# Tying two modulation units behind the last activation of each feed-forward part

## The chip, the cores and the metric

The kernel runs on one core of one Trainium2 chip. TensorE (PE) multiplies matrices, VectorE (DVE) and ScalarE (ACT) work element by element, GpSimd (POOL) does little here, and SyncE (SP) issues the transfers (DMA) that bring weights from the chip's main memory into the core's own. Each engine works through its own list of instructions in order; semaphores tie the lists together. The metric is the time of one execution on the device in microseconds (us). The kernel before takes 2133.24 us, the median of three runs (2132.33 to 2133.75).

## What is computed

The reference is an encoder trunk of two layers on 512 tokens of width 1024. Each layer is a feed-forward half-step, a token mixer and another feed-forward half-step; the mixer is a state-space scan in the first layer and differential attention in the second. Cut to what matters here:

```python
cond = silu(c)
for i in range(DEPTH):
    mods = (cond @ ada_w[i] + ada_b[i]).reshape(b, N_SUB, 3, D_MODEL)
    gate = lambda s: (1 + mods[:, s, 2])[:, None, :]
    y = swiglu(modulate(x, mods[:, 0]), ffn_w_gate[i, 0], ffn_w_up[i, 0], ffn_w_down[i, 0])
    x = layer_norm(ALPHA * x + 0.5 * gate(0) * y, ln_g[i, 0], ln_b[i, 0])
    ...
    y = swiglu(modulate(x, mods[:, 2]), ffn_w_gate[i, 1], ffn_w_up[i, 1], ffn_w_down[i, 1])
    x = layer_norm(ALPHA * x + 0.5 * gate(2) * y, ln_g[i, 2], ln_b[i, 2])
```

with `swiglu(u) = (silu(u @ w_gate) * (u @ w_up)) @ w_down`, D_FF = 2816.

## The kernel before

**Arithmetic.** Everything is float32, but TensorE is fed a rounded format (F32R). Each operand x is therefore split into a high part (ScalarE copies x into the rounded format) and a low part (VectorE subtracts the high part from x), and each product is three matmuls: high by high, high by low, low by high (`mm3`, L182). So every weight and every activation costs ScalarE one instruction and VectorE one: L123 and L126 for weights, L155 and L156 for activations (`split_act`, which calls `split_into`).

**The feed-forward layers** (`ffn`, called with n = 0, 2, 3 and 5; here the first to the fourth feed-forward layer). The 2816 hidden columns are 22 blocks of 128, in three parts of 8, 7 and 7 blocks. In a part, the kernel first makes the activations of its blocks one after another and appends their split forms to the list `hs`; then come eight down units (`down_units`), one for each 128 output columns. A down unit loads its weight, splits it, multiplies it with all activations of the part (7 or 8 blocks by three matmuls, the last activation last in program order), and adds the result to the residual (L415). The first ten blocks of the first layer and the first four of the others are done by plain projections; the remaining ones by `seven`, a scheme with seven half-size products in place of eight. Its weights are added and split on VectorE and ScalarE (`weight_forms`, L543, L544 and L553), and its activation comes out of a short chain: L590 on VectorE, a SiLU on ScalarE (L591), a product on VectorE (L592), and the split. The inputs of `seven` need split sums of the layer's input as well (`input_forms`); these are made beside the last four plain blocks, and they too go through `split_act`.

**The modulation units** (`ada_unit`, L207). The vector `mods` is computed on VectorE, off the matmul path: one unit loads 128 rows of 1024 weights (512 KB), multiplies them with the conditioning vector and sums along the row, one instruction and a short one that reads the sum. There are 72 units for each of the trunk's two layers. A generator issues them a few at a time: in the first feed-forward layer two after each down unit of the first two parts and one after each of the third; in the second and the third layer two after each down unit of the first two parts; some others beside the activations. The fourth has none.

**Buffers and loads** (`load`, L99). All weights, those of the modulation units too, go through one kind of buffer. Four belong to one pool; inside the feed-forward layers every fifth load uses a buffer of its own. SyncE issues the loads. A buffer is free again once the last instruction that reads it has run: the split of a weight, or the modulation unit itself.

**What sets the order.** The order of each engine's list is not that of the program text. A planner at compile time goes through the instructions by their place in the program, with costs for each, and gives an engine the next instruction that is ready in its own simulated time. So a modulation unit whose weights have come early, while VectorE has nothing else ready, is put ahead of work that stands before it in the program. An order can be forced with `add_manual_dep(a, b, NOSYNC)`: a is not put ahead of b. Between two instructions of one engine that needs no semaphore.

Of the kernel before, what the change touches and what calls it, by code (L numbers as in the profile page):

```python
# [43 lines left out]
NOSYNC = mybir.DependencyInfo(mybir.DependencyClass.NoSync, mybir.DependencyReason.DATA)  # L44


def hybrid_trunk(tc, xT, cb, par, cst, adaw, wgu, wdn0, wdn1, wdn2, wdt, win, wso, wqk, wv, wao, dist_in, dtp, lam_in, out):
    nc = tc.nc
# [13 lines left out]
    def big(dt=F32, name="big"):  # L62
        return ap.tile([P, T], dt, tag="a", name=name)

    def tmp(name="tmp"):
        return tp.tile([P, T], F32, tag="t", name=name)

    def acc(tag="acc"):
        return ps.tile([P, T], F32, tag=tag, name=tag, bufs=BANKS[tag])
# [19 lines left out]


    fifth, at, last_load, hold_split = [None], [0], [None], [None]

    def load(src, n=1024):
        at[0] = (at[0] + 1) % 5
        if fifth[0] is not None and at[0] == 0:
            raw = fifth[0].tile([P, 1024], F32, tag="raw5", name="raw", bufs=1)
        else:
            raw = wp.tile([P, 1024], F32, tag="raw", name="raw", bufs=4)
        last_load[0] = nc.sync.dma_start(raw[:, :n], src)  # L99
        return raw[:, :n]  # L100
# [46 lines left out]

    def split_act(src, scale=None):
        hi, lo = big(F32R, "hi"), big(F32R, "lo")
        split_into(hi, lo, src, scale)  # L150
        return hi, lo

    def split_into(hi, lo, src, scale=None):
        if scale is None:
            x = nc.scalar.activation(hi, src, AF.Copy)  # L155
            y = nc.vector.tensor_tensor(out=lo, in0=src, in1=hi.bitcast(F32), op=ALU.subtract)  # L156
            return x, y
        else:
            nc.scalar.activation(hi, src, AF.Copy, scale=scale)
            nc.vector.scalar_tensor_tensor(  # L160
                out=lo, in0=src, scalar=scale, in1=hi.bitcast(F32), op0=ALU.mult, op1=ALU.subtract
            )
# [30 lines left out]
    def proj(o, w, u, m=P, cols=FULL, prev=None, lows_last=False):  # L193
        for a, b in cols:
            prev = mm3(
                o[:m, a:b], [(w[k][0], w[k][1], u[k][0][:, a:b], u[k][1][:, a:b]) for k in range(len(u))], prev,
                lows_last=lows_last,
            )
        last_mm[0] = prev
        return prev  # L200
# [3 lines left out]

    def ada_unit(l, j):
        raw = load(adaw[l, j])
        nc.vector.scalar_tensor_tensor(  # L207
            out=raw, in0=raw, scalar=1.0, in1=cond, op0=ALU.mult, op1=ALU.mult,
            accum_out=mods[l][:, j : j + 1],
        )  # L210

    onep, shift, gvec, lnG, lnB, lnag, lnab = {}, {}, {}, {}, {}, {}, {}

# [34 lines left out]
    def ada_stream(l, js):  # L248
        for j in js:
            ada_unit(l, j)  # L250
            if (j + 1) % 8 == 0:
                s, ty = divmod(j // 8, 3)
                n = l * 3 + s
                if ty == 1 and n > 0:
                    make_shift_scale(n)
                elif ty == 2:
                    make_gate(n)
            yield

    def advance(g, n):  # L260
        for _ in range(n):
            if g is None or next(g, "end") == "end":
                return
# [145 lines left out]
    def scale_residual(k=KT):  # L409
        for f in later[:k]:  # L410
            f()
        del later[:k]

    def add_res(d, pd, n, a, b):
        nc.vector.scalar_tensor_tensor(  # L415
            out=res[d][:, a:b], in0=pd[:, a:b], scalar=gvec[n][:, d : d + 1], in1=res[d][:, a:b],
            op0=ALU.mult, op1=ALU.add,
        )
# [3 lines left out]
    def first_units(n):  # L422

        if n == 1:
            src = [win[e] for e in range(2)]
        elif n == 4:
            src = [wqk[0, e] for e in range(2)]
        else:
            src = [wgu[{2: 1, 3: 2, 5: 3}[n], j // 2, j % 2] for j in range(3)]
        return [split(load(x), "a") for x in src]  # L430

    def down_units(n, u, units, ln=None, KEEP=4):

        last = ln is not None
        keep = []
        for ld in units:
            for d, w in ld():
                if last and d >= KT - KEEP:
                    keep.append((d, w))
                    continue  # L440
                pd = acc()
                proj(pd, w, u)
                add_res(d, pd, n, 0, T)
                if last:
                    ln.feed(d, 0, T)
            yield
        if last:
            finish(n, ln, [(d, w, u) for d, w in keep])

    def finish(n, ln, keep, begun={}):  # L450

        norm = None
        for a, b in HALVES:
            for d, w, u in keep:
                if a == 0 and d in begun:
                    pd, k0 = begun[d]
                    last_mm[0] = mm3(pd[:, a:b], [(*w[k], *(x[:, a:b] for x in u[k])) for k in range(k0, len(u))], start=False)
                else:
                    pd = acc()
                    proj(pd, w, u, cols=((a, b),))  # L460
                add_res(d, pd, n, a, b)
                ln.feed(d, a, b)
                advance(norm, 2)
            advance(norm, KT)
            norm = ln.normalize(a, b, ln.stats(a, b))
        advance(norm, KT)
        next_u[0] = ln.u
        ln.residual()
# [127 lines left out]
    def ffn(n, stream=None, per=(0, 0, 0), pre=None, first7=FT):  # L596


        forms, making = [], None
        ln, shifting = LN(n), None  # L600
        sc = ExitStack()
        extra[0] = fifth[0] = sc.enter_context(tc.tile_pool(name=f"wx{n}", bufs=3))
        idx = {0: 0, 2: 1, 3: 2, 5: 3}[n]
        u = next_u[0]
        f = 0
        pre = pre or first_units(n)
        for pi, nf in enumerate(FPARTS):
            hs = []
            open7 = None
            for _ in range(nf):  # L610
                if f >= first7:
                    g = seven(load(wgu[idx, f, 0]), load(wgu[idx, f, 1]), forms, hs)
                    next(g)
                    advance(shifting, 1)
                    if open7 is not None:
                        next(open7, None)
                    next(g)
                    open7 = g
                    f += 1
                    continue  # L620
                wg, wu = (pre.pop(0) if pre else split(load(wgu[idx, f, e])) for e in range(2))
                cols = HALVES if f < 2 and n > 0 else FULL
                tag = "mid" if f == 2 else "ln" if f == 3 and n == 0 else "acc"
                pg = acc(tag)
                proj(pg, wg, u, cols=cols, lows_last=f < 1 and n > 0)
                pu = acc(tag)
                proj(pu, wu, u, cols=cols, lows_last=f < 1 and n > 0)
                sg = tmp("sg")
                nc.scalar.activation(sg, pg, AF.Silu)
                h = tmp("h")  # L630
                nc.vector.tensor_tensor(out=h, in0=sg, in1=pu, op=ALU.mult)
                hs.append(split_act(h))
                if first7 - 4 <= f < first7:
                    making = making or input_forms(u)
                    forms.append(next(making))
                f += 1
                scale_residual(2 if f < 5 else KT)
                if f > 3 or n > 0:
                    advance(stream, per[0])

            if open7 is not None:
                next(open7, None)

            def mk(d):
                return lambda: [(d, split(load(wdn[pi][idx, d], nf * P)))]

            for _ in down_units(n, hs, [mk(d) for d in range(KT)], ln if pi == len(FPARTS) - 1 else None):
                advance(stream, per[1 if pi < 2 else 2])
            if pi == len(FPARTS) - 2:
                shifting = ln.shift()  # L650
        extra[0] = fifth[0] = None
        sc.close()
# [612 lines left out]
    for d in range(KT):  # L1265
# [9 lines left out]
        for o in (hl[0], uf):  # L1275
            x = nc.scalar.activation(o, res[d], AF.Identity, bias=shift[0][:, d : d + 1], scale=onep[0][:, d : d + 1])
# [8 lines left out]
    next_u[0] = up  # L1285
    st0 = ada_stream(0, range(16, 72))
    ffn(0, st0, (2, 2, 1), [[k[j] for k in ks] for j in range(8)], first7=10)
    advance(st0, 100)
    ssm(1)
# [108 lines left out]
```

## Time and profile before

| | |
|---|---|
| median of three runs | 2133.24 us |
| the profiled execution | 2134.65 us |
| its span, first to last instruction | 2132.8 us |
| TensorE busy in the span | 2099.9 us |
| VectorE busy | 1770.3 us |
| ScalarE busy | 1093.8 us |
| modulation units on VectorE, 144 of them | 173.7 us |

All are of one execution except the median. "Busy" of TensorE counts a matmul from its start to a modelled end, and matmuls overlap. The granted clock of TensorE was 0.997 of full speed in this execution. In the views below, a row of a timeline reads: start in us from the span's start, length in us, engine, line, operation, output and inputs by the program's names, shapes, count, and in brackets the engine's idle time before it with what ended it. A row of the chain of waits reads: start, length, what the end of the program was waiting for at that time. A row of a list of waits reads: who waited for whom, us in total, how often, the longest. The row of a group reads: line, engine, operation, names, shapes, count, then busy time in us, mean length in ns, and the engine's idle time before it. Of a transfer it gives KB each and the median time from issue to landing in us.

### The profile page before, as it was taken

How to read it: one execution, taken by the hardware profiler on the slowest of the kernel's cores; microseconds unless marked ns; L12 is line 12 of the kernel's file. 1: busy time of each engine (PE TensorE's matmuls, PEld its weight loads, DVE VectorE, ACT ScalarE, POOL GpSimd, SP SyncE). 2: the span in 40 equal slices, each digit the busy share in tenths (PEclk: the TensorE clock that was granted, in tenths of full speed). 3: DMA queues.
4: the chain of work that ended last, by engine and by line, in shares of the span. 5: the costliest groups of instructions: out<-in, count | busy, mean ns of one | idle time of the engine just before them, and what ended most of it. 6: DMA issues, size and time to landing. Idle time of an engine off the chain costs nothing.

```text
span 2132.8 us, 34111 instructions
## 1 busy us (share of the span) xinstructions
PE 2099.9 (98%) x13234; PEld 1854.1 (87%) x13234; DVE 1770.3 (83%) x2932; ACT 1093.8 (51%) x1833; POOL 180.6 (8%) x258
## 2 busy tenths in 40 slices
PE   7999999999999999999999999999999999999998
PEld 6889899976777699899999989899988888989897
DVE  6979998677667898989988989997788889858796
ACT  5424354777656646343456434353866647424343
POOL 0000000056333400000000000000011100000000
PEclk9999999999999999999999999999999999999999
DMA  8863735375554352727343373723322322323231
GB/s 321 306 227 99 247 97 195 93 214 170 151 152 135 92 159 72 271 91 238 123 144 104 106 240 103 253 96 113 92 69 80 90 81 78 124 75 119 71 118 40
DMA packets 90274, 301.19 MB, mean 141 GB/s; under 512 B 10240, under 2 KB 13696, under 8 KB 90112
## 3 DMA queue, kind: packets, MB, share of 16 engines
q1 hardware_dynamic: 88576, 294.81, 42.6%
q0 software_dynamic: 1536, 4.20, 0.9%
q8 instruction: 104, 1.70, 0.3%
q14 instruction: 58, 0.48, 0.1%
HBM read 289.53 MB, written 5.24 MB: 138 GB/s over the span
## 4 chain that ended last, share of the span: by engine, by line
PE 85%; DVE 7%; DMA 2%; issue 2%; ACT 2%; POOL 1%; SPq 0%; POOLq 0%; ACTq 0%; DVEq 0%
PE acc L182 68%; PE mid L182 9%; PE mid L909 2%; PE mid L1142 1%; DVE raw L207 1%; PE ln L182 1%; DMA raw<-in_adaw 1%; DVE raw L553 1%; DVE wl L544 1%; DMA raw<-in_wdn 1%; PE ln L1164 1%; PE ln L847 0%; POOL E L899 0%; DVE wl L126 0%; PE ln L339 0%
## 5 line engine op out<-in xcount | busy, mean ns | idle before, releaser
L182 PE MATMUL acc<-hi,wh 128*128 128x256 f32 (+1 forms) x1568 | 522.0, 334 | 1.8 <-ACT hi L155 1.8
L182 PE MATMUL acc<-lo,wh 128*128 128x256 f32 (+1 forms) x1568 | 521.8, 333 | 0.6 <-DVE lo L156 0.6
L182 PE MATMUL acc<-hi,wl 128*128 128x256 f32 (+1 forms) x1568 | 520.6, 333 | 0.0
L182 PE MATMUL acc<-uh,wh 128*128 128x256 f32 (+1 forms) x1160 | 391.7, 339 | 0.0
L182 PE MATMUL acc<-uh,wl 128*128 128x256 f32 (+1 forms) x1160 | 386.6, 335 | 0.0
L182 PE MATMUL acc<-ul,wh 128*128 128x256 f32 (+1 forms) x1160 | 384.0, 335 | 0.0
L123 ACT ACTIVATE wh<-raw 128x1024 fp32r<-128x1024 f32 (+1 forms) x210 | 212.4, 1022 | 278.3 <-PE acc L182 109.6
L543 ACT ACTIVATE wh<-raw 128x1024 fp32r<-128x1024 f32 x198 | 209.3, 1059 | 255.2 <-DVE raw L553 115.2
L182 PEld LDWEIGHTS acc<-hi,wh 128*128 128x128 f32 x1568 | 295.9, 189 | 35.9 <-ACT hi L155 5.2
L182 PEld LDWEIGHTS acc<-lo,wh 128*128 128x128 f32 x1568 | 296.3, 189 | 31.0 <-DVE lo L156 2.4
L182 PEld LDWEIGHTS acc<-hi,wl 128*128 128x128 f32 x1568 | 296.0, 189 | 29.2
L126 DVE TENSOR_TENSOR wl<-raw,wh 128x1024 fp32r<-128x1024 f32 (+1 forms) x210 | 248.4, 1188 | 49.3 <-ACT wh L123 46.7
L544 DVE TENSOR_TENSOR wl<-raw,wh 128x1024 fp32r<-128x1024 f32 x198 | 240.9, 1219 | 22.5 <-ACT wh L543 21.0
L182 PEld LDWEIGHTS acc<-uh,wh 128*128 128x128 f32 x1160 | 219.1, 189 | 28.3 <-issue 6.4
L182 PEld LDWEIGHTS acc<-uh,wl 128*128 128x128 f32 x1160 | 219.1, 189 | 22.7 <-issue 0.4
L182 PEld LDWEIGHTS acc<-ul,wh 128*128 128x128 f32 x1160 | 217.5, 189 | 21.9 <-issue 0.6
L553 DVE TENSOR_TENSOR raw<-raw 128x512 f32<-128x512 f32 x264 | 181.3, 688 | 4.9
L207 DVE SCALAR_TENSOR_TENSOR raw<-raw,cond 128x1024 f32<-128x1024 f32 x144 | 173.7, 1218 | 10.5 <-DMA raw<-in_adaw 10.3
L415 DVE SCALAR_TENSOR_TENSOR resid<-acc,gv,resid 128x512 f32<-128x512 f32 (+1 forms) x156 | 104.5, 672 | 82.7 <-PE acc L182 82.1
L353 POOL TENSOR_TENSOR rr<-vr,mhalf 128x2 f32<-128x2 f32 x12 | 8.4, 698 | 1515.6 <-DVE vr L349 1515.6
L182 PE MATMUL mid<-uh,wh 128*128 128x256 f32 (+2 forms) x332 | 99.2, 301 | 0.5 <-DVE up L585 0.5
L182 PE MATMUL mid<-uh,wl 128*128 128x256 f32 (+2 forms) x332 | 99.0, 299 | 0.0
(268 smaller groups left out, 3926.0 us busy)
## 6 DMA issues: line engine op xcount, KB each, us to landing
raw<-in_wgu SPq DMA_DIRECT2D x176, 512.0 KB, 4.0
raw<-in_adaw SPq DMA_DIRECT2D x144, 512.0 KB, 4.7
raw<-in_wdn SPq DMA_DIRECT2D x64, 448.0 KB, 4.1
raw<-in_win SPq DMA_DIRECT2D x40, 512.0 KB, 4.0
raw<-in_wdn SPq DMA_DIRECT2D x32, 512.0 KB, 4.5
rw<-scr SPq DMA_DIRECT2D x32, 512.0 KB, 6.0
ch<-scr SPq DMA_DIRECT2D x32, 256.0 KB, 6.2
raw<-in_wso SPq DMA_DIRECT2D x16, 512.0 KB, 4.3
```

The source lines that it names most:

```text
L123: x = nc.scalar.activation(hi[:, :n], raw, AF.Copy)
L126: nc.vector.tensor_tensor(out=lo[:, :n], in0=raw, in1=hi[:, :n].bitcast(F32), op=ALU.subtract)
L182: last = nc.tensor.matmul(o, lhsT=a, rhs=b, start=start and j == 0, stop=j == len(pairs) - 1, skip_group_check=not start)
L207: nc.vector.scalar_tensor_tensor(out=raw, in0=raw, scalar=1.0, in1=cond, op0=ALU.mult, op1=ALU.mult, accum_out=mods[l][:, j : j + 1],)
L353: nc.gpsimd.tensor_tensor(out=r[:, :m], in0=vr[:, :m], in1=mhalf[:, :m], op=ALU.pow)
L415: nc.vector.scalar_tensor_tensor(out=res[d][:, a:b], in0=pd[:, a:b], scalar=gvec[n][:, d : d + 1], in1=res[d][:, a:b], op0=ALU.mult, op1=A ...
L543: nc.scalar.activation(x[0], r, AF.Copy)
L544: nc.vector.tensor_tensor(out=x[1], in0=r, in1=x[0].bitcast(F32), op=ALU.subtract)
L553: nc.vector.tensor_tensor(out=o, in0=x, in1=y, op=ALU.add)
L909: x = nc.tensor.matmul(py[hh * 64 : (hh + 1) * 64, cc], lhsT=lhs, rhs=rhs, start=k == 0, stop=k == 2)
L1142: nc.tensor.matmul(ss[m], lhsT=q[:, c], rhs=qks[h, 1][m], start=j == 0, stop=j == 1)
L1164: gated(nc.tensor.transpose(pw[:, k * P : (k + 1) * P], w[:, k * P : (k + 1) * P], ident))
```

## The change

`split_act` now remembers what `split_into` returned, the instructions that make the high and the low part. When a part's activations are made and before its down units, `part_end` is set to the low part of the last split. Modulation units issued while `part_end` is set get a NOSYNC dependence on it. It is cleared after the first down unit's turn, so that the tie holds for the units of that turn alone: two in each of the first two parts of the first three feed-forward layers, and one in the third part of the first. The splits of the down weights get no such tie.

In the first part of the first layer the last block is one of those that make an input form beside it. The split that `last_act` remembers there is the last one of that input form, not that of the activation.

```diff
+    last_act, part_end = [None], [None]
...
     def split_act(src, scale=None):
         hi, lo = big(F32R, "hi"), big(F32R, "lo")
-        split_into(hi, lo, src, scale)
+        last_act[0] = split_into(hi, lo, src, scale)
         return hi, lo
...
     def ada_unit(l, j):
         raw = load(adaw[l, j])
-        nc.vector.scalar_tensor_tensor(
+        x = nc.vector.scalar_tensor_tensor(
             out=raw, in0=raw, scalar=1.0, in1=cond, op0=ALU.mult, op1=ALU.mult,
             accum_out=mods[l][:, j : j + 1],
         )
+        if part_end[0]:
+            tc.add_manual_dep(x.ins, part_end[0].ins.name, NOSYNC, reason="last activation of the part first")
...
+            part_end[0] = last_act[0][1]
             for _ in down_units(n, hs, [mk(d) for d in range(KT)], ln if pi == len(FPARTS) - 1 else None):
                 advance(stream, per[1 if pi < 2 else 2])
+                part_end[0] = None
```

## The prediction

> **What bounds the kernel now.** I read the page first, then the list of waits on TensorE, then the chain of waits and the timeline around each place that the change touches.
>
> ```profile
> span 2132.8 us, 34111 instructions
> PE 2099.9 (98%) x13234; PEld 1854.1 (87%) x13234; DVE 1770.3 (83%) x2932; ACT 1093.8 (51%) x1833; POOL 180.6 (8%) x258
> PE 85%; DVE 7%; DMA 2%; issue 2%; ACT 2%; POOL 1%; SPq 0%; POOLq 0%; ACTq 0%; DVEq 0%
> L207 DVE SCALAR_TENSOR_TENSOR raw<-raw,cond 128x1024 f32<-128x1024 f32 x144 | 173.7, 1218 | 10.5 <-DMA raw<-in_adaw 10.3
> raw<-in_adaw SPq DMA_DIRECT2D x144, 512.0 KB, 4.7
> raw<-in_wdn SPq DMA_DIRECT2D x64, 448.0 KB, 4.1
> ```
>
> TensorE sets the end: 2099.9 of 2132.8 us, 85% of the chain. An edit that leaves the matmuls alone can win only from the 2132.8 - 2099.9 = 32.9 us in which TensorE is idle. A modulation unit (L207) costs VectorE 1.22 us and TensorE nothing. It matters only where VectorE's order makes a matmul wait. Which waits are those? From the list of waits on TensorE:
>
> ```profile
> PE acc L182 <- ACT wah L115: 11.4, 1, 11.4
> PE acc L182 <- ACT hi L155: 1.8, 3, 0.8
> PE acc L182 <- DVE lo L156: 0.6, 1, 0.6
> ```
>
> The 11.4 us is one wait at the start of the program. The next two rows are matmuls that waited for the high or the low part of an activation: four waits, 1.8 + 0.6 = 2.4 us in all. Each stands at the end of a feed-forward part: the second part of the first feed-forward layer, the first part of the second one, and both streamed parts of the third. There the first down unit has used up the older activations and wants the last one. The first of them on TensorE's timeline (start, length, then the idle time before it):
>
> ```profile
> 224.33 0.39 PE L182 MATMUL acc<-lo,wh 128*128 128x512 f32 x1
> 224.56 0.40 PE L182 MATMUL acc<-hi,wl 128*128 128x512 f32 x1
> 225.65 0.73 PE L182 MATMUL acc<-hi,wh 128*128 128x512 f32 x2 [0.70 <-ACT hi L155]
> ```
>
> Matmuls of this shape start 224.56 - 224.33 = 0.23 us apart, so the wait lost 225.65 - 224.56 - 0.23 = 0.86 us of issue time, 0.16 more than the idle time shown, as an ending is modelled after the next start. With 0.16 added to each, the four waits cost 2.4 + 4 x 0.16 = 3.0 us. That is 0.14% of 2133.24. About 0.2%, or 4.3 us, is what a measurement of this kernel can tell from no change; so all that the change aims at lies inside that bound.
>
> **What the change moves.** It adds no instruction, DMA or semaphore: VectorE runs both the low part and the unit, so the tie is an order on one engine. In seven places (three parts of the first feed-forward layer, two each of the second and third) the modulation units issued after the first down unit, 13 in all, may come only behind the last low part. The units keep their 13 x 1.22 us on VectorE. Where do they stand now? The units between 200 and 262 us, one row for all, and VectorE's timeline at that part's end:
>
> ```profile
> L207 DVE SCALAR_TENSOR_TENSOR raw<-raw,cond x16: 1214/1217/1223, 199.8 to 242.4; 128x1024 f32<-128x1024 f32 x16
> 222.00 1.22 DVE L207 SCALAR_TENSOR_TENSOR raw<-raw,cond 128x1024 f32<-128x1024 f32 x1
> 223.14 0.69 DVE L592 TENSOR_TENSOR sg<-sg,up 128x512 f32<-128x512 f32 x1
> 223.75 1.22 DVE L207 SCALAR_TENSOR_TENSOR raw<-raw,cond 128x1024 f32<-128x1024 f32 x1
> 225.63 0.69 DVE L156 TENSOR_TENSOR lo<-sg,hi 128x512 fp32r<-128x512 f32 x1 [0.66 <-ACT hi L155]
> 226.24 1.08 DVE L126 TENSOR_TENSOR wl<-raw,wh 128x896 fp32r<-128x896 f32 x1
> ```
>
> These 16 are the units of that part's eight down units. The two that get tied are the first two: they run at 199.8 and just after, 26 us ahead of the low part at 225.63. The ones that stand in the last activation's way, at 222.00 and 223.75, are later ones, which stay free. So the tie does not take these away directly. It works through the buffers: a tied unit keeps its weight buffer until it has run, and there are five (four in one pool, and every fifth load uses one of its own). Two held buffers leave three to pass on the loads behind them, so fewer later units have landed by the time the last activation is due. That is why I expect the units in the way to thin out, not to vanish.
>
> Now each wait, from the chain of waits in its own window (start, length, what). The first, at 225.65:
>
> ```profile
> 218.97 5.08 DMA raw<-in_wdn
> 224.13 0.96 ACT wh L123
> 225.08 0.52 ACT hi L155
> ```
>
> Not a modulation unit but a down weight's split holds the high part up. ScalarE works in order; its weight split had waited for a load that took 5.08 us, and the high part stood behind it. Splits stay free, so this wait can stay. The second, and its row from the waits in 870 to 890 us:
>
> ```profile
> PE acc L182 <- ACT hi L155: 0.3, 1, 0.3
> 879.42 0.26 DVE raw L207
> 880.48 0.08 DVE raw L207
> 880.90 1.13 DVE wl L126
> 882.67 0.64 ACT hi L155
> ```
>
> Here two modulation units and a weight's low part stand in VectorE's queue ahead of the last activation; one unit (1.22 us) fewer covers the wait of 0.3 + 0.16 = 0.5. The third, at 1239.75:
>
> ```profile
> 1232.37 5.39 DMA raw<-in_adaw
> 1237.86 1.23 DVE raw L207 x2
> 1239.09 0.61 DVE lo L156
> 1239.75 1.89 PE acc L182 x7
> ```
>
> This is the case that the change is about: VectorE waits for a modulation weight that took 5.39 us to land, runs that unit, and only then the low part. With two buffers held, this unit (the eighth of its sixteen) is not yet loaded; the wait of 0.6 + 0.16 = 0.8 goes. The fourth:
>
> ```profile
> 1346.10 5.09 DMA raw<-in_wdn
> 1351.27 0.95 ACT wh L123
> 1353.29 0.64 ACT hi L155
> 1353.97 3.08 PE acc L182 x12
> ```
>
> It is of the first kind again: ScalarE sits behind a down weight's load. Its idle time is the 0.8 of the list. I leave it in place.
>
> So the sum is -0.5 - 0.8 = -1.3 us; its bounds are 0 (other units fill the freed slots of VectorE) and -3.0 (all four waits go).
>
> What is late next, and what does the moved work cost? Two tied units now follow the low part, 2 x 1.22 = 2.4 us, and, by my estimate (two of five buffers held, so two fifths of the six units now between them and the low part, rounded up), three later units, 3.7 us. Queued behind them on VectorE are the next down weight's low part and the additions into the residual, then the preparation of the next part's weights. Two rows bound that, the busy times of the engines in the down units of this part (stretch, its length, then PE, PEld, DVE, ACT and POOL) and the last weight prepared in it, against the matmul that needs it:
>
> ```profile
> 225.50:264.00 38.50, 38.35 (x186) 32.21 (x187) 34.58 (x48) 11.99 (x15) 0.00 (x0) 1.00 0.70 248
> 260.05 1.22 DVE L544 TENSOR_TENSOR wl<-raw,wh 128x1024 fp32r<-128x1024 f32 x1 [0.17 <-ACT wh L543]
> 272.23 0.28 PE L182 MATMUL mid<-hi,wh 128*128 128x256 f32 x1
> ```
>
> VectorE has 38.50 - 34.58 = 3.9 us free there, and the weight split at 260.05 is done 272.23 - 261.27 = 11 us before it is read. About 6 us more of units fits into 3.9 + 11. I take 0 for it; without that cover it would cost 6.1 - 3.9 = 2.2 us a place.
>
> The trace cannot show how long the three free buffers take to pass the down weights. Below, it could gain: fewer loads in flight may land sooner. This view of the weight buffers' loads gives the spread:
>
> ```profile
> DMA to landing us min/median/max: 3.0/4.2/12.6
> ```
>
> A load that lands in 3.0 instead of 5.09 us would remove the fourth wait, and 5.08 the first. The Trainium skill, in "DMA: Bandwidth & Descriptors", section "Latency and other measured facts", says that access to HBM takes 0.2 us on average and 2 us at high load, so that a lighter load shortens a transfer's fixed cost; by that, a waiting load could land up to 1.8 us sooner, which would cover all four waits and make the sum -3.0. The trace agrees in the spread (3.0 to 5.09), but does not show that load is its cause. Above, it could cost: see the slower rival. I take 0, as the pattern of the loads is nearest to what it was.
>
> The profiled execution took 2134.65 us, 1.85 around its span, and 1.4 above the median 2133.24 of the runs. The same -1.3 gives 2133.35 for such an execution and 2133.24 - 1.3 = **2131.9 us** for the median.
>
> **Rivals.**
>
> All four waits go: 2133.24 - 3.0 = 2130.2. For it: the two waits on a down weight hang on loads of over 5 us, slow against a median of 4.2. Against it: the splits that wait for them are left free.
>
> Nothing comes of it: 2133.2. The change would not do what it says, in effect: the tied units were never the ones in the way (199.8 against 225.63), and the third to eighth run as before. Against it: the held buffers must slow the later loads.
>
> Slower: the held buffers starve the down weights. Place: the third down unit of a part. If the three free buffers are filled by later units that VectorE has not reached by the end of the low part at 225.63 + 0.69 = 226.3, the third weight's load goes out only when a unit has run, at 227.5; it lands at 227.5 + 4.1 = 231.6, and its two parts (0.96 and 1.08) are ready at 233.6. TensorE wants it after two units: 21 matmuls of 0.23 us are 4.8 for the second, begun at about 226.4, so at 231.2. That is 2.4 us for each place, 17 for all seven; it decides for slower from two places on. Half of them give 2133.2 + 3.5 x 2.4 = 2141.6. For it: the tied units hold their buffers for about 26 us. Against it: a down weight stands ahead of the units that follow it in the program, and today's loads are early: the row at 218.97 is the fifth down weight of its part, wanted at 226.4 + 3 x 4.8 = 240.8, 22 us later. The first part of the first layer is the likeliest place, since there the last activation split is that of an input form, later than the last activation itself.
>
> Much faster: a thinner queue on VectorE also removes waits outside the parts' ends, over 4.3 us in all, say 2133.24 - 5 = 2128.2. Against it: TensorE's listed waits at these places sum to 3.0.
>
> **How the numbers follow.** Chances: my forecast 0.42, all four waits 0.16, nothing 0.25, slower 0.12, much faster 0.05. The first three lie within 0.2%: 0.83. The range must hold 2130.2 and 2133.2 with the runs' own spread of about 0.7 us, and one starved place with a lost cover (2.2 + 2.4 = 4.6 above the forecast): 2129.2 to 2136.5. It leaves out the much faster case and the larger part of the slower one.
>
> **What would show it.** At each of the seven places the profile after should have the low part of the last activation ahead of two units of L207 that now start before it, and fewer units of L207 in the ten microseconds before it. TensorE's wait for the low part (0.6) should be gone, that for the high part should be near 1.5. The preparation of the next weights should come a few microseconds later, with no wait of TensorE on it. I am wrong if the chain at these places shows a load of a down weight that went out after the low part, if the units before the low part are as many as now, or if TensorE waits somewhere in the mixers where it did not.

## The result and the profile after

The change makes the kernel slower: 2158.2 us, median of five runs (2153.72 to 2161.56), against 2132.33 for the kernel before in the same five rounds. The ratio is 1.0121, 95% interval 1.011 to 1.0131, so 1.2% and 25.9 us. The profiled execution took 2157.39 us, 22.7 more than the profiled one before; the views below are of these two. The page of the profile after, its span, busy times, shares of the chain, and the rows of the modulation units and their transfers:

```profile
span 2155.6 us, 34090 instructions
PE 2107.6 (98%) x13234; PEld 1856.1 (86%) x13234; DVE 1774.3 (82%) x2932; ACT 1092.0 (51%) x1833; POOL 178.3 (8%) x258
PE 73%; DVE 13%; DMA 6%; ACT 3%; issue 3%; POOL 1%; SPq 0%; ACTq 0%; POOLq 0%; DVEq 0%
L208 DVE SCALAR_TENSOR_TENSOR raw<-raw,cond 128x1024 f32<-128x1024 f32 x144 | 174.2, 1219 | 21.9 <-DMA raw<-in_adaw 21.5
raw<-in_adaw SPq DMA_DIRECT2D x144, 512.0 KB, 4.5
raw<-in_wdn SPq DMA_DIRECT2D x64, 448.0 KB, 4.0
```

(One line was added above L99, and further ones below: L207 is now L208, L123 is L124, L155 and L156 are L156 and L157.) The same 13234 matmuls and the same units of 1.22 us; no engine has more to do. VectorE and the transfers have grown in the chain, from 7% and 2% to 13% and 6%: TensorE waits for them. VectorE waited 21.5 us for modulation weights, against 10.3. A transfer, once issued, takes no longer (4.5 against 4.7 us). The waits on TensorE in the profile after:

```profile
PE acc L183 <- ACT wah L116: 11.5, 1, 11.5
PE acc L183 <- ACT wh L124: 4.5, 2, 4.3
PE acc L183 <- ACT hi L156: 3.7, 5, 1.1
PE acc L183 <- ACT sg L585: 3.7, 6, 1.4
PE ln L313 <- ACT z L312: 2.9, 2, 1.6
```

The wait for the low part (0.6 before) has gone. That for the high part has doubled (1.8 to 3.7), and three kinds are new: for a down weight's split (L124), for a SiLU of a part's last activations (L585), and for the first step of the layer norm's shift (L312), which runs after a part's down units.

Where are these places? TensorE runs the same number of matmuls in both kernels, so one can set the start of the n-th matmul in the one trace against that in the other. The table gives by how much this lag grows in each place, in us, and the same for four experiments told below. Here and below, "first layer" to "fourth layer" mean the feed-forward layers.

| place | after | e1_hold | e4_act | e5_own | e8_first_place |
|---|---|---|---|---|---|
| first layer, first part | +7.3 | +6.8 | 0.0 | 0.0 | +7.0 |
| first layer, second part | +3.4 | +1.2 | +3.2 | -1.0 | -0.2 |
| first layer, third part | +1.8 | +0.8 | +2.1 | +0.6 | -0.6 |
| second layer, first part | +1.9 | +0.7 | +5.1 | -0.6 | +0.6 |
| second layer, second part | +2.5 | +5.4 | +2.9 | +2.1 | 0.0 |
| third layer, first part | +1.0 | +1.1 | +1.2 | -0.1 | 0.0 |
| third layer, second part | +4.0 | +0.9 | +3.7 | +1.5 | -1.2 |
| lag near the end | 22.6 | 17.7 | 19.5 | 2.0 | 6.7 |

In the column "after" the seven places give 21.9 of 22.6 us. Between them, in the sevens and in both mixers, the lag moves by 0.2 us or less each time, and by 0.4 us over the fourth layer. So the cost is local, at the ends of the parts, where the change acts.

**The first place.** VectorE's timeline and then SyncE's, of the profile after:

```profile
113.68 0.68 DVE L157 TENSOR_TENSOR lo<-fb,hi 128x512 fp32r<-128x512 f32 x1
114.28 1.22 DVE L208 SCALAR_TENSOR_TENSOR raw<-raw,cond 128x1024 f32<-128x1024 f32 x1
115.42 1.22 DVE L208 SCALAR_TENSOR_TENSOR raw<-raw,cond 128x1024 f32<-128x1024 f32 x1
122.46 1.21 DVE L208 SCALAR_TENSOR_TENSOR raw<-raw,cond 128x1024 f32<-128x1024 f32 x1
```

```profile
116.68 2.13 SPq L100 DMA_DIRECT2D raw<-in_adaw  x2
119.63 2.61 SPq L100 DMA_DIRECT2D raw<-in_wgu  x2
123.71 0.33 SPq L100 DMA_DIRECT2D raw<-in_wdn  x1
```

The two tied units run right behind the input form's low part, as ordered. Counted through `load` in the order of the program, the second of them holds the fifth buffer, which takes every fifth load: next the modulation weight five loads later, then the fifth down weight five after that. The chain can be read off the rows. The second tied unit is through at 115.42 + 1.14 = 116.56, and a modulation load goes out at 116.68; when that has landed and its unit has run (at 122.46), the down weight's load goes out at 123.71. In the profile before the fifth down weight had gone out at 97.13. TensorE's timeline:

```profile
124.55 0.39 PE L183 MATMUL acc<-hi,wl 128*128 128x512 f32 x1
129.24 0.80 PE L183 MATMUL acc<-hi,wh 128*128 128x512 f32 x1 [4.31 <-ACT wh L124]
129.84 0.63 PE L183 MATMUL acc<-lo,wh 128*128 128x512 f32 x1
135.26 0.39 PE L183 MATMUL acc<-hi,wh 128*128 128x512 f32 x1
```

It wanted that weight at 124.8 and got it at 129.24: 129.24 - 124.55 - 0.23 = 4.5 us lost. And the matmul behind the wait takes 0.80 us, not 0.39. By stretches (length, then PE, PEld, DVE, ACT and POOL busy, the granted clock of TensorE, the transfers' share and GB/s):

```profile
124.50:129.20 4.70, 0.43 (x2) 0.01 (x1) 2.62 (x5) 2.12 (x3) 0.00 (x0) 0.90 0.75 266
129.20:132.00 2.80, 2.76 (x7) 2.18 (x8) 2.78 (x3) 1.88 (x2) 0.00 (x0) 0.50 0.66 202
132.00:135.00 3.00, 3.00 (x9) 2.32 (x8) 2.34 (x4) 0.00 (x0) 0.00 (x0) 0.50 0.92 324
135.00:140.00 5.00, 5.00 (x23) 4.07 (x22) 2.18 (x8) 1.06 (x1) 0.00 (x0) 0.99 0.87 293
```

The granted clock stands at 0.50 from the end of the wait until about 135. From 129.24 to 135.26, in 6.0 us, TensorE started 14 matmuls, most of them 0.43 us apart; at 0.23 us they take 3.2 us. That is the other 2.8 of the 7.3 us.

**The other places** lose time in another way. The last one, from the chain of waits:

```profile
1353.61 5.89 DMA raw<-in_adaw
1359.52 1.24 DVE raw L208 x2
1360.76 0.35 DVE px L593
1361.13 0.02 ACT sg L594
1361.45 0.94 ACT wh L124
1362.42 1.09 DVE wl L127
```

```profile
1366.77 4.03 DMA raw<-in_wdn
1370.88 0.96 ACT wh L124
1371.86 1.09 DVE wl L127
1372.95 0.60 DVE lo L157
```

Each engine's list is fixed before the run. Here VectorE's list has a modulation unit ahead of a step of the last activations, and ScalarE's has a down weight's split ahead of the SiLU that TensorE waits for. The down weights' loads went out late. The one issued at 1366.77 went out at 1346.10 in the profile before; of these 20.7 us, 18.2 are the lag that the profile after had gathered by then, and 2.5 are new. The three down weights before it in this part are 3.3 to 6.7 us late by the same reckoning. The engines stood still in front of these loads. But the modulation load at 1353.61 is not late: before it went out at 1336.22, which with the lag is 1354.4. Here the order itself has changed. In VectorE's list before, the step of the activation stands ahead of that unit; after, the unit stands ahead of the step (L208 ahead of L593 in the rows above). The rows of before:

```profile
1340.26 0.41 DVE L590 TENSOR_TENSOR px<-px,mid 128x256 f32<-128x256 f32 x1
1342.76 1.23 DVE L207 SCALAR_TENSOR_TENSOR raw<-raw,cond 128x1024 f32<-128x1024 f32 x1 [0.29 <-DMA raw<-in_adaw]
```

So in this place late loads and a new order of the list both have a part; how much each costs was not told apart. Further on, at 1411, the layer norm's shift is late because the next part's weight preparation on VectorE and ScalarE has started late:

```profile
1408.91 0.70 DVE raw L556
1409.72 1.06 ACT wh L546
1411.05 0.53 ACT z L312
```

### The profile page after: what moved, and what is told of

It is laid out like the page before. It is cut to its first block, busy times and chain, and to the rows that moved or that the text cites. A ratio compares the mean times of both kernels' runs of the same rounds, so it can differ in the third digit from the quotient of the medians.

```text
span 2155.6 us, 34090 instructions
## 1 busy us (share of the span) xinstructions
PE 2107.6 (98%) x13234; PEld 1856.1 (86%) x13234; DVE 1774.3 (82%) x2932; ACT 1092.0 (51%) x1833; POOL 178.3 (8%) x258
## 4 chain that ended last, share of the span: by engine, by line
PE 73%; DVE 13%; DMA 6%; ACT 3%; issue 3%; POOL 1%; SPq 0%; ACTq 0%; POOLq 0%; DVEq 0%
PE acc L183 57%; PE mid L183 8%; DVE raw L556 3%; DMA raw<-in_adaw 3%; DVE raw L208 3%; DMA raw<-in_wdn 2%; DVE wl L547 2%; PE mid L914 2%; PE mid L1147 1%; PE ln L183 1%; DVE wl L127 1%; DMA raw<-in_wgu 1%; ACT wh L124 1%; ACT wh L546 1%; DVE lo L157 1%
## 5 line engine op out<-in xcount | busy, mean ns | idle before, releaser
L124 ACT ACTIVATE wh<-raw 128x1024 fp32r<-128x1024 f32 (+1 forms) x210 | 212.4, 1021 | 298.5 <-PE acc L183 121.3
L547 DVE TENSOR_TENSOR wl<-raw,wh 128x1024 fp32r<-128x1024 f32 x198 | 240.4, 1218 | 21.8 <-ACT wh L546 20.7
L183 PEld LDWEIGHTS acc<-uh,wl 128*128 128x128 f32 x1160 | 219.2, 189 | 22.7 <-issue 0.4
L208 DVE SCALAR_TENSOR_TENSOR raw<-raw,cond 128x1024 f32<-128x1024 f32 x144 | 174.2, 1219 | 21.9 <-DMA raw<-in_adaw 21.5
```

The costliest lines, as they stand in the source:

```text
L124: x = nc.scalar.activation(hi[:, :n], raw, AF.Copy)
L183: last = nc.tensor.matmul(o, lhsT=a, rhs=b, start=start and j == 0, stop=j == len(pairs) - 1, skip_group_check=not start)
L208: x = nc.vector.scalar_tensor_tensor(out=raw, in0=raw, scalar=1.0, in1=cond, op0=ALU.mult, op1=ALU.mult, accum_out=mods[l][:, j : j + 1],)
L547: nc.vector.tensor_tensor(out=x[1], in0=r, in1=x[0].bitcast(F32), op=ALU.subtract)
```

## The experiments

Two theories. The buffers theory: the tied units keep two of the five weight buffers until the last low part, so the loads behind them go out late, and in-order engines stand in front of them. The order theory: the units' own work, moved behind the low part, makes VectorE late for the next down weights and the next part. All ratios are to the kernel before, run beside the experiments (2131.8 to 2132.4 us).

**e1_hold: the buffers are held, the units are not moved.**

```diff
-            tc.add_manual_dep(x.ins, part_end[0].ins.name, NOSYNC, ...)
+            x = nc.vector.tensor_scalar(out=held, in0=raw[:, 0:1], scalar1=1.0, scalar2=None, op0=ALU.mult)
+            tc.add_manual_dep(x.ins, part_end[0].ins.name, NOSYNC, ...)
```

> Every modulation unit runs where the planner likes, as in the kernel before; but the 13 units' weight buffers are kept until after the last low part, by one tiny extra instruction each (128x1 on VectorE, tied behind the low part). Buffers theory (the cost of the change is that two of five weight buffers stay held, so that the loads behind them come late): most of the loss stays, 2148 to 2160 us. Order theory (the cost is the units' own 1.22 us each, now run after the low part, ahead of down-weight splits and of the next part's weights): 2130 to 2137 us, since no unit is moved.

Measured: 2154.53 us, ratio 1.0107 (1.0092 to 1.0122). The first place shows the same wait of TensorE as the change, without a tied unit. Two of its rows of waits:

```profile
PE acc L183 <- ACT wh L124: 4.0, 1, 4.0
PE acc L183 <- ACT hi L156: 3.7, 6, 0.9
```

Thirteen instructions of 0.15 us, which only read a buffer late, cost 22.7 us. This lies in the range of the buffers theory: with the units left free, holding the buffers alone brings most of the 25.9 us. Place by place the match is looser. Outside the first place e1_hold loses 10.1 us and the change 14.6; in the second part of the second layer it is 5.4 against 2.5, in the last place 0.9 against 4.0 (table).

**e2_late: the loads of the tied units ordered behind the low part too.**

```diff
             tc.add_manual_dep(x.ins, part_end[0].ins.name, NOSYNC, ...)
+            tc.add_manual_dep(last_load[0].ins, part_end[0].ins.name, NOSYNC, ...)
```

> The change, and the loads of the 13 tied units are ordered by the planner behind the same low part, so that they hold no buffer while they wait; the units still run after the low part. Buffers theory: the loss goes, 2129 to 2138 us. Order theory: the units run as late as in the change or later, so 2150 to 2160 us.

Measured: 2178.16 us, ratio 1.0217 (1.0201 to 1.0232): neither theory's number. The trace shows that the edit did not do what it was meant to. SyncE's timeline in the first place, and its longest wait there:

```profile
83.11 2.14 SPq L100 DMA_DIRECT2D raw<-in_adaw  x2
110.04 0.33 SPq L100 DMA_DIRECT2D raw<-in_wdn  x1
```

```profile
SPq L100 <- DVE raw L208: 29.1, 6, 24.7
```

The edge is the planner's alone; nothing on the chip holds the load back. So the tied loads still went out early, while the units stood further back, as the planner took the loads to come late (its reasoning is not in the trace): four units ran from 108.8 us on, with one down weight's low part between them, and with all buffers full no load went out for 110.04 - 85.25 = 24.8 us. As a test of the theories it fails; as it came out, it is a case with more buffers held and a larger loss.

**e3_own and e5_own: an extra buffer for the tied units.** In both the tied units load into a buffer of their own; they differ in where its 4 KB come from.

```diff
+        if part_end[0]:
+            at[0] = (at[0] + 1) % 5
+            raw = fifth[0].tile([P, 1024], F32, tag="tied", name="raw", bufs=1)
+            nc.sync.dma_start(raw, adaw[l, j])
+        else:
+            raw = load(adaw[l, j])
```

> The change, but the 13 tied units load into one extra buffer of their own, so that all five of the ring stay free for the others (to make room, the squares of the layer norm have one buffer in place of two). Buffers theory: 2129 to 2138 us. Order theory: 2150 to 2160 us.

Measured: 2158.16 us, ratio 1.0115 (1.0098 to 1.0131). That would speak for the order theory, but the loss is elsewhere: at the end of the first layer the lag is 0.0 us, and 12.1 us come at one layer norm, near 1510 us, where this kernel has one buffer less for the squares; most of the rest comes in the two mixers. In the seven places together the lag grows by 1.5 us. Its edit also moved the count of the fifth buffer in all loads, so the total tells nothing apart.

> The change, with one extra buffer for the 13 tied units, so that none of the five ring buffers is held; this time the room comes from the layer norm's sums (two buffers in place of three) and the squares keep their two. The count that picks the fifth buffer runs on as in the change. Buffers theory: 2128 to 2137 us, the four waits of before partly gone. Order theory: 2150 to 2160 us, since the units run after the low part as in the change.

Measured: 2136.62 us, ratio 1.0018 (1.0009 to 1.0027). This is in the range of the buffers theory: the units run after the low part, and 21.5 of the 25.9 us have gone. In the first place nothing is left (table). One difference from the change weakens the test of the order theory. The two units of a place share the one buffer, so the second's load goes out only when the first has run, and that unit runs later: in the first place at 114.23 and 120.07, where the change has 114.28 and 115.42. Only one of the two stands right behind the low part; a run with two extra buffers was not made. TensorE's wait for the high part of an activation:

```profile
PE acc L183 <- ACT hi L156: 3.0, 3, 1.4
```

TensorE still waits three times, 3.0 us against 1.8 before. From the chain of waits at the second part of the third layer:

```profile
1350.03 4.87 DMA raw<-in_wdn
1354.99 0.95 ACT wh L124
1355.93 0.53 ACT hi L156
```

It is a down weight's split in front of the high part, as in two of the four waits of before.

**e6_sums2: the control.** The kernel before with the smaller layer norm buffers of e5_own (`bufs=2` for the tag "l").

> The kernel before with two buffers in place of three for the layer norm's sums: the control of e5_own. Both theories: within 3 us of before, 2130 to 2135.

Measured: 2131.03 us, ratio 0.9998 (0.9988 to 1.0007): no difference. So against its control, e5_own loses 5.6 us.

**e4_act: in the first place the tie is to the activation, not the input form.**

```diff
+            kept = last_act[0]
             (th, tl), (bh, bl) = split_act(top), split_act(bot)
+            last_act[0] = kept
```

> The change, but in the first part of the first feed-forward layer the tie is to the last activation's low part instead of the last input form's, which comes 6.7 us later in the profile after. If the 4.5 us wait of TensorE there and the half clock behind it (2.8 us) come from the fifth buffer being held until that later instruction, they go: 2151 us, 7 below the change. If any held buffer costs the same there, 2157 or more.

Measured: 2153.58 us, ratio 1.0101 (1.0086 to 1.0116). In the first place the lag is 0.0, as the fifth-buffer chain has it: the wait and the half clock are both gone. The clock there, from the stretches:

```profile
124.00:130.00 6.00, 6.00 (x28) 4.89 (x27) 6.00 (x9) 1.06 (x1) 0.00 (x0) 1.00 0.88 314
```

The whole gained 4.6 us, not 7, since the first part of the second layer lost 5.1 instead of 1.9. TensorE's timeline and the stretch behind it show what the 5.1 us are:

```profile
883.64 0.58 PE L183 MATMUL acc<-hi,w4h 128*128 128x256 f32 x1 [2.15 <-ACT sg L587]
883.70:887.10 3.40, 3.40 (x14) 3.30 (x15) 3.19 (x8) 1.06 (x1) 0.00 (x0) 0.51 0.54 154
```

TensorE waited 2.15 us for a SiLU that stood behind a down weight's split on ScalarE (the weight's load had gone out at 876.01), and ran at half clock for the 3.4 us behind it. Half of 3.4 is 1.7, so the two make about 4 of the 5.1 us; the rest was not traced further.

**e7_one: one unit tied in each place.** `part_end` is cleared after the first unit.

> The change with one unit tied in each place instead of two (7 units instead of 13), so one buffer is held, and never the fifth buffer in the first layer's first part. Buffers theory: the cost falls faster than the number of units, because three of the seven microseconds' worst place hang on the fifth buffer: 2134 to 2145 us. Order theory: half the loss, 2143 to 2147.

Measured: 2142.98 us, ratio 1.006 (1.0041 to 1.0078). In the range of the buffers theory, but also at the edge of the order theory's; it tells little apart. The first place loses nothing here too: the one tied unit does not hold the fifth buffer.

**e8_first_place: the change in the first place alone.** `part_end` is set only for `n == 0 and pi == 0`.

> The change in the first part of the first feed-forward layer alone; the other six places as before. Both theories have the wait of 4.5 us and the 2.8 us at half clock in this place: 2132 + 7.3 = 2139 us, and nothing later, if the places are independent of each other. If moving one place makes the planner reorder later ones, 2143 or more.

Measured: 2142.17 us, ratio 1.0051 (1.0036 to 1.0066), so 9.9 us against an expected 7.3, between the two forecasts. In its trace the first place costs 7.0 and the others together -1.4; the lag near the end is 6.7. Of the 3.2 us between 6.7 and 9.9, 2.3 come from the profile of before that it is set against, an execution 2.3 us over the median 2132.33, and 0.9 from its own, which is 0.9 us under its median.

**e9_sixth: a sixth buffer, no tie.**

```diff
-        at[0] = (at[0] + 1) % 5
+        at[0] = (at[0] + 1) % (5 if extra[0] is None else 3)
...
-            raw = fifth[0].tile([P, 1024], F32, tag="raw5", name="raw", bufs=1)
+            raw = fifth[0].tile([P, 1024], F32, tag="raw5", name="raw", bufs=1 if extra[0] is None else 2)
```

> No tie: the kernel before with a sixth weight buffer in the feed-forward layers (two of the second kind, every third load; room from the layer norm's sums as in e6_sums2). If held buffers cost time because loads come late, a free one more should not cost, and may win what the four waits at the parts' ends cost: 2127 to 2132 us. If the planner's order is only unlucky whenever it is disturbed, 2136 or more.

Measured: 2145.64 us, ratio 1.0059 (1.0045 to 1.0073): outside the range of the buffers theory, and in that of the other forecast, by which any disturbed order loses. Until 1009 us the trace is within 4 us of before, mostly ahead of it; then 10.7 us come at the end of the second layer, where its layer norm meets the third layer's first weights (1144.7 to 1152.0 us of the profile before). A spare buffer does not win the waits at the parts' ends, and it upsets another place. Why there was not settled. So an edit that holds no buffer can cost 13.2 us too, and a kernel's total alone does not show why it is slower. What ties the change's loss to the buffers is that it sits in the seven places (table), that e1_hold brings most of it back there, and that e5_own takes most of it away there.

**e10_own6: six units tied in a place, all through the extra buffer.** As e5_own, with `part_end` cleared after the third down unit.

> e5_own with the units of the first three down units tied, six in a place instead of two, all through the one extra buffer. Buffers theory with the later units in the way: those six are the ones that stood ahead of the low part, so the waits on VectorE's queue go and only those on a down weight's split stay: 2128 to 2135 us. If the moved work itself costs (the 4 us that e5_own still lost with two units), three times as much: 2142 to 2150.

Measured: 2140.76 us, ratio 1.0043 (1.0029 to 1.0056): between the two. Tying the units that really stood in the way, with no ring buffer held, leaves the high part's waits at 1.9 us, against 1.8 before, and costs 8.3 us; three times the 4.4 of e5_own would be 13. This is not the price of the order alone: the six units share one buffer, and SyncE's queue stands in front of their loads for 80.9 us in all, against 14.3 in e5_own.

**e11_splits: no unit tied; ScalarE's splits of the third to sixth down weight behind the last high part.**

```diff
+            high, turns = last_act[0][0] if n > 0 or pi > 0 else None, 0
             for _ in down_units(...):
+                hold_split[0] = None
                 advance(stream, per[1 if pi < 2 else 2])
-                part_end[0] = None
+                turns += 1
+                hold_split[0] = high if 2 <= turns < 6 else None
+            hold_split[0] = None
```

> No tie of modulation units; instead ScalarE's splits of the third to sixth down weight are ordered behind the last high part, in all parts but the first of the first layer. These are the instructions that ScalarE stood in at two of the four waits of before. If those waits are all: minus 1.8, 2129 to 2132 us. If a later split frees its weight buffer later and so delays the loads behind it: 2136 to 2150.

Measured: 2132.57 us, ratio 1.0003 (0.9994 to 1.0012): nothing. The high part's waits fall from 1.8 to 1.2 us, and another takes their place: its list of waits has

```profile
PE mid L183 <- DVE up L588: 2.1, 1, 2.1
```

## Why the prediction was wrong

Forecast 2131.9, range 2129.2 to 2136.5; measured 2158.2. By its own steps:

**The bound and the prize: borne out.** TensorE still sets the end, the places are the seven named, and nothing that was tried won any of the 3.0 us at stake there: e5_own, e10_own6 and e11_splits each remove some waits and get others. Of the two waits that made the forecast's -1.3, that for the low part has gone, and so has that for the high part in the first part of the second layer; but there are five waits for a high part now, 3.7 us in all, where about 1.5 were expected.

**The tie holds: borne out.** The tied units run directly behind the low part (114.28 and 115.42 in the first place), and the wait for a low part is gone. The thinning of the units in between was small: in the second part of the first layer three units start in the ten microseconds before the last low part, against four.

**The step that failed** is the price of the held buffers: "The trace cannot show how long the three free buffers take to pass the down weights ... I take 0, as the pattern of the loads is nearest to what it was." Held buffers cost 22.7 us in e1_hold, with no unit tied. The prediction's own sign of being wrong came true: in the first place the load of a down weight went out at 123.71, after the low part at 113.68. The expected thinning and the cost are one mechanism: a load that comes too late to be in the way also comes too late for the engine whose list already has it ahead of the activation. The prediction took the thinning as a gain and gave the same delay no price.

**The slower rival had the mechanism and the likeliest place, not the size.** It gave "held buffers starve the down weights" a chance of 0.12, 2.4 us a place and 17 for all seven. Six places lost 1.0 to 4.0 us, 14.6 in all; the first lost 7.3. It named the third down weight; in the first place it was the fifth, through the fifth buffer. That chain was in the prediction's reach: from the low part's end at 112.22 + 0.69 = 112.9 in the profile before, two units (2 x 1.22), a load (4.7), a unit (1.22) and a load of a 512 KB down weight (4.5) make 125.8, with the split's high part (1.06) 126.8, against the 124.6 at which TensorE begins its fifth down unit there. That is a wait of about 2.2 us in one place, where the forecast had 0.

**What no part of the prediction had** is the half clock. The wait of 4.5 us cost 2.8 more behind it, and one of 2.15 us was followed by 3.4 us at 0.51 (e4_act). The profile before already shows it once, in the first mixer, behind a wait of 2.50 us on TensorE:

```profile
497.12 1.22 PE L822 MATMUL ln<-xc 128*128 128x256 f32 x2 [2.50 <-ACT bt L816]
497.10:500.50 3.40, 3.38 (x10) 2.82 (x11) 1.85 (x3) 2.44 (x6) 0.72 (x1) 0.50 0.33 90
```

The Trainium skill, "TensorE: Matmul & The Clock Gate", under "Part 1: The HAM clock gate", has the clock go to half after at least one idle window of about 3.4 us, and back after one such window of work. For the return the 3.4 us behind the wait of 2.15 agree, and the 6 us or so in the first place are more than one window. For the fall the runs differ from the page: 2.15 us sufficed.

**The cover for the moved work** held better than the rest, but was not whole. The prediction took 0 for it. e5_own, with the buffers free, lost 5.6 us against its control, and e10_own6 9.7 (its control ran in other rounds). I put this down to the changed lists of VectorE, ScalarE and SyncE; this is argued, not shown: the instruction is known only for single waits, not for the sum.

Not settled: what sets the size of each wait. The second part of the second layer costs 2.5 us in the change, 5.4 in e1_hold and 2.1 in e5_own. Part of this spread is the clock, as TensorE's timeline and the stretch behind it in e1_hold show:

```profile
1048.09 0.50 PE L316 MATMUL ln<-z,onesn 128*128 128x512 f32 x1 [1.94 <-ACT z L315]
1049.50:1052.90 3.40, 3.40 (x19) 3.40 (x18) 3.25 (x3) 1.26 (x2) 0.00 (x0) 0.51 0.60 202
```

But why the wait arises in the one kernel and not in the other stays open: the planner's lists differ after each edit, and no run held them fixed.

## What to carry to other kernels

An instruction that reads a buffer of a shared ring has a second cost beside its duration: the time for which it keeps the buffer. Before tying it to something late, list the loads that come next into the same ring, follow them to the engine that stands in order in front of them, and do so for each kind of buffer by the count that assigns it. And if a wait of 2 us or more can arise on TensorE, add the half clock behind it to the upper end of the price.

## What the runs showed of the hardware

A wait of 4.5 us on TensorE was followed by about 6 us of matmuls at a granted clock of 0.50 (0.43 us between starts of matmuls that take 0.23). Shorter waits were followed by one stretch of 3.4 us at half clock in some places and by none in others: 2.50 us in the kernel before, 2.15 us in e4_act and 1.94 us in e1_hold by one, but 2.19 us in e8_first_place (at 504.81) and 1.97 us in e5_own by none, as e5_own's timeline and the stretch behind the wait show:

```profile
511.42 0.87 PE L919 MATMUL mid<-E,xt 128*64 128x256 f32 x6 [1.97 <-DVE E L910]
511.40:515.00 3.60, 3.58 (x21) 2.57 (x22) 3.53 (x5) 2.93 (x7) 3.60 (x6) 1.00 0.18 54
```

So the length of a wait alone does not decide it near 2 us; what else does was not tested.

Loads landed hardly sooner with fewer free buffers: the median was 4.5 us against 4.7 for the modulation weights, and 4.0 against 4.1 for the down weights of 448 KB.
